# Handing every transfer but weights, first loads and last stores from SyncE's queue to GpSimd's

## The chip, the cores and the metric

The kernel runs on one core of a Trainium2 chip. The metric is the device time of one execution in microseconds (us). Within a core, TensorE (PE), VectorE (DVE), ScalarE (ACT), GpSimd (POOL) and SyncE (SP) each work through a list of instructions of their own in a fixed order. An instruction that waits holds up all that stand behind it on its engine. SP only issues transfers; an issue on any engine sets a transfer going and its landing is told by a semaphore.

## The reference

A two-layer decoder trunk runs over 512 prompt tokens and 8 sample tokens, width 1024, all in float32:

```
for l in 0, 1:
    x = x + 0.5 * rms_norm(swiglu(rms_norm(x)))          # FFN A, inner width 2816
    proj = rms_norm(x) @ w_in                            # q f i g | gu gv | su | gates
    a, hgrn_state = hgrn2(xq, xf, xi, xg, state)         # 4 heads, 128x128 state each
    b, v_rows     = gmlp(gu, gv)                         # 128x128 position mixing
    c, s5_state   = s5(su, state)                        # complex diagonal SSM, 512 wide, then GLU
    merged = sum over branches of sigmoid(gates) * (branch @ w_branch)
    x = x + rms_norm(merged @ w_out)
    x = x + 0.5 * rms_norm(swiglu(rms_norm(x)))          # FFN B
```

The outputs are x after layer 1 and the new states of the three mixers for both token groups.

## The kernel before

The activations stay in SBUF, transposed, in two halves of 256 and 264 columns. Every weight matrix is streamed once: `unit` (L95) loads a block of 128x1024 into one of three `raw` buffers (L102, on SP), ACT rounds it to `whi` (L103) and DVE, for a few blocks POOL, makes the rest `wlo` (L107, L237). `mm3` (L118) multiplies each block in three passes (L122, L123, L125), so that PE has some 20,000 of these matmuls, and they are the bulk of the work.

The order of the instructions on each engine is made when the program is built, by a scheduler that reads the Python code and interleaves it; on the chip it is fixed. Side jobs are written as Python generators that are stepped while the main matmuls are laid down (`tick`, L963). Three of them matter here.

- **The tables.** During FFN A of layer 0, `s5_tables` (L533) computes from the S5 parameters 16 sets of four tables (`s5_table`, L641), 8 for each layer. POOL does most of the arithmetic (L504 to L509, L665 to L667, L683 to L688); PE does four small products a set (L695) that need POOL's `er` and `ei` (L667). Each set is stored to DRAM by four transfers (L711), and a load `bc` (L549) brings the input of a later one.
- **The scan.** At the start of each mixer `s5_project` (L735) writes the S5 input to DRAM and reads it back in another layout (L771 to L779). Then `s5_scan` (L781) makes eight steps. Each loads its four tables (`table`, L792 to L796; tables 0, 1 and 2 have one buffer each), PE projects with table 0 (L803), DVE runs the recurrence, POOL fills edge columns of `w` (L827 to L830), and PE multiplies with tables 2 and 1 (L857 to L859). Every second step goes through DRAM once more (L867, L870).
- **The HGRN heads.** `hgrn_head` (L1035) loads sample states and broadcast values (L1118, L1121) and stores new states (L1129, L1186).

All 920 transfers are issued by SP. Besides the weights these are 496: x in and out, the side jobs' loads and stores, and a spill of x at the middle of each layer (L359) that is read back near the mixer's end (L1348).

Of the kernel before, what the change touches and what calls it, by code (L numbers as in the profile page):

```python
# [45 lines left out]
class Trunk:  # L46
# [29 lines left out]
    def load_consts(self):  # L76
        nc, t, c = self.nc, self.t, self.const
        self.mask = c.tile([P, 64 + 3 * SEGS * 32], U8, name="mask")
        with self.tc.tile_pool(name="mkp", bufs=1) as pool:
            m = pool.tile([P, 64 + 3 * SEGS * 32], F32, name="m")  # L80
            nc.sync.dma_start(m, t["level_mask"])
            nc.gpsimd.tensor_copy(self.mask, m)
        self.tri = c.tile([P, P], F32, name="tri")
        nc.sync.dma_start(self.tri, t["tri_mask"])
        self.hg = c.tile([P, DEPTH * 4], F32, name="hg")
        nc.sync.dma_start(self.hg, t["hgrn_norm_g"])
        self.glub = c.tile([P, DEPTH * 8], F32, name="glub")
        nc.sync.dma_start(self.glub, t["glu_b"])


    def gcol(self, l, i, j, half=False):
# [251 lines left out]
    def residual(self, half, r1, y2, x2, pre, spill):  # L343
        nc, v, sl, w = self.nc, self.nc.vector, SL[half], HW[half]
        if pre is not None and half == 0:
            self.new_h()
        acc = self.acc2_room()[:, :, :w] if pre is not None else None
        for q in range(KD // 2):
            t, xs = y2[q][:, :, sl], x2[q][:, :, sl]
            v.tensor_tensor(t, t, r1[:, None].to_broadcast([P, 2, w]), ALU.mult)  # L350
            v.tensor_tensor(xs, t, xs, ALU.add)
            for e in range(2):
                j = 2 * q + e
                if pre is None:
                    nc.sync.dma_start(self.t["y"][j][:, sl], xs[:, e])
                    continue
                self.pre_hi(*pre, half, j)
                if spill is not None:
                    nc.sync.dma_start(spill[j][:, sl], xs[:, e])  # L359
            if pre is not None:  # L360
                yield
        if pre is None:
            return
        for q in range(KD // 2):
            xs = x2[q][:, :, sl]
            self.pre_lo(*pre, half, 2 * q)
# [144 lines left out]
    def lower_bounds(self):  # L511

        nc, c = self.nc, self.const
        with self.tc.tile_pool(name="lbp", bufs=1) as pool:
            z = pool.tile([P, DEPTH, 4], F32, name="lb_z")
            nc.sync.dma_start(z, self.t["lb_logits"])
            e = pool.tile([P, DEPTH, 4], F32, name="lb_e")
            base = pool.tile([P, DEPTH, 4], F32, name="lb_base")
            m = pool.tile([P, 4], F32, name="lb_m")
# [13 lines left out]
    def s5_tables(self, pool):  # L533
# [12 lines left out]

        def load(i):
            bc = pool.tile([P, 4, 2, 32], F32, tag="bc", name="bc", bufs=3)
            nc.sync.dma_start(bc, self.t["s5_bc"][i // 8, i % 8])  # L549
            return bc  # L550

        n = 8 * DEPTH
# [16 lines left out]
    def s5_params(self, pool, NPR, k):  # L569
# [5 lines left out]
        nc.sync.dma_start(lr, t["lam_re"])  # L575
        nc.sync.dma_start(li, t["lam_im"])
        nc.sync.dma_start(ld, t["log_dt"])
        nc.sync.dma_start(k["d"], t["s5_d"])
# [62 lines left out]
    def s5_table(self, pool, l, s, k, rc, bc):  # L641
# [66 lines left out]
                        k["d"][:, cc][:, :, None].to_broadcast([P, 2, P]), ALU.mult)  # L708
        v.tensor_tensor(m3f, m3f, dd, ALU.add)
        for i in range(4):  # L710
            nc.sync.dma_start(dst[i], tb[i])  # L711
        self.tab.append(dst)
        yield

# [20 lines left out]
    def s5_project(self, l, f_block, ev_f):  # L735
# [32 lines left out]
        for m in range(4):  # L768
            d = self.dr.tile([P, 4, NT // 4], F32, tag="ud", name="ud", bufs=4)
            ds = self.dr.tile([P, NS], F32, tag="us", name="us", bufs=4)  # L770
            nc.sync.dma_start(d, ups[m])  # L771
            nc.sync.dma_start(ds, uss[m])
            ub = self.ub[m]
            nc.gpsimd.memset(ub[:, :, 128:], 0.0)
            dv = d.rearrange("(q c) j n -> j c q n", q=4)
            for j in range(4):
                nc.sync.dma_start(ub[32 * j:32 * j + 32, :, :128], dv[j][:, :, :128])
            for j, c in ((3, 128), (0, 136)):
                nc.sync.dma_start(ub[32 * j:32 * j + 32, :, c:c + NS], ds.rearrange("(q c) n -> c q n", q=4))  # L779

    def s5_scan(self, l, pool):  # L781

# [4 lines left out]
        nc.sync.dma_start(st, t["state_s5"][l])  # L787
# [26 lines left out]
        for s in range(n):  # L814
# [49 lines left out]
                self.gelu2(zb[:, lp + a], pt[:, a * NB:(a + 1) * NB], self.tmp, "sil", 2)  # L864
            if lp == 2:
                d = self.dr.tile([P, 4 * NB], F32, tag="zd", name="zd", bufs=4)
                nc.sync.dma_start(d, zb.rearrange("p q n -> p (q n)"))  # L867
                dv = d.rearrange("(j c) (q n) -> q c j n", j=4, q=4)
                for k in range(4):
                    nc.sync.dma_start(zz[32 * k:32 * k + 32], dv[k])  # L870
                z = self.xp.tile([P, 2, NT], F32R, tag="x", name="z")
                zh, zl = z[:, 0], z[:, 1]
                for d0, src in ((lambda a: a[:, :NP].rearrange("p (n j) -> p n j", j=4),
                                 zz[:, :, :128].rearrange("p j n -> p n j")),
                                (lambda a: a[:, NP:], zz[:, 0, 136:144])):
# [8 lines left out]
        for k, (x0, x1, op) in enumerate(((st[:, 0], st[:, 1], ALU.subtract), (st[:, 1], st[:, 0], ALU.add))):  # L884
# [4 lines left out]
        nc.sync.dma_start(t["s5_sample"][l], new)  # L889
        nc.sync.dma_start(t["s5_prompt"][l], fin)  # L890

    def s5_glu(self, l):
        nc, t = self.nc, self.t
# [90 lines left out]
    def hgrn_values(self, l, hh, pool, V):  # L984
# [10 lines left out]
                                     scale=self.rc[:n, i:i + 1])  # L995

        self.tok_proj("w_i", l, hh, evac)
        nc.sync.dma_start(vd, vs)
        for e in range(2):
            V[2 * hh + e] = v4[e], vd[:, e]  # L1000

# [33 lines left out]
    def hgrn_head(self, l, h, V, q0, qs, k, f, sg, pool, last):  # L1035
# [79 lines left out]

        def load(b0):
            st = pool.tile([P, 2, P], F32, tag="st", name="st", bufs=2)
            nc.sync.dma_start(st, t["state_hgrn"][l, h][:, b0:b0 + 2])  # L1118
            vb = pool.tile([P, 2, P], F32, tag="vb", name="vb", bufs=2)
            for b in range(2):  # L1120
                nc.sync.dma_start(vb[:, b], vd[b0 + b].partition_broadcast(P))  # L1121
            loaded.append((st, vb))

        def state(b0):
            st, vb = loaded.pop(0)
            for b in range(2):
                nc.scalar.activation(st[:, b], st[:, b], AF.Copy, scale=fs[:, b0 + b:b0 + b + 1])
                v.scalar_tensor_tensor(st[:, b], vb[:, b], ks[:, b0 + b:b0 + b + 1], st[:, b], ALU.mult, ALU.add)
            nc.sync.dma_start(t["hgrn_sample"][l, h][:, b0:b0 + 2], st)  # L1129
            states.append((b0, st))  # L1130

        def output():
# [47 lines left out]
        for i in range(4):  # L1180
# [5 lines left out]
        nc.sync.dma_start(t["hgrn_prompt"][l, h], S[3])  # L1186
        yield
        po = self.pxt()
        for i in range(4):
# [38 lines left out]
    def gmlp_norm(self, l, pool):  # L1228
        nc, t, vt = self.nc, self.t, self.vt
        v, g = nc.vector, nc.gpsimd  # L1230
        ng, nb = pool.tile([P, 512], F32, name="ng"), pool.tile([P, 512], F32, name="nb")
        nc.sync.dma_start(ng, t["gmlp_ng"][l])
        nc.sync.dma_start(nb, t["gmlp_nb"][l])
        stat = pool.tile([P, 5, 2], F32, name="stat")
        v.memset(stat, 1.0)
        for i in range(5):
# [9 lines left out]
        for i in range(5):  # L1246
# [5 lines left out]
        nc.sync.dma_start(t["gmlp_v"][l], vt[4][:NS])  # L1252

    def gmlp_mix(self, l, pool, fill):

        nc, t, vt = self.nc, self.t, self.vt
        v, g = nc.vector, nc.gpsimd
        ws = pool.tile([P, 4, P], F32, name="ws")
        nc.sync.dma_start(ws, t["gmlp_ws"][l])
        bs = pool.tile([P, 4, P], F32, name="bs")  # L1260
        nc.sync.dma_start(bs, t["gmlp_bs"][l])
        w00 = pool.tile([NS, 4], F32, name="w00")
        nc.sync.dma_start(w00, t["gmlp_w00"][l])
# [31 lines left out]
    def mixer(self, l, xd, finish, ahead):  # L1295
# [46 lines left out]
        with tc.tile_pool(name=f"mh{l}", bufs=KD) as mh:  # L1342
# [180 lines left out]
```

## Time and profile before

| | |
|---|---|
| median of 3 runs | 2705.61 us (2705.0 to 2705.9) |
| the profiled execution | 2704.64 us, of which the span from first to last instruction 2702.8 us |
| PE busy, matmuls | 2640.5 us, 98% |
| DVE, ACT, POOL busy | 59%, 39%, 21% |
| mean granted PE clock | 0.993 |

Busy is the time in which an engine had an instruction running. PE's 98% says that little of the span is left for waits; the shares of the others are means over stages that differ much: POOL is near full in the tables' stage and almost idle in the FFNs.

### The profile page before, as it was taken

What the parts mean: (1) busy time and instruction counts of PE and PEld (TensorE: products, weight loads), DVE (VectorE), ACT (ScalarE), POOL (GpSimd) and SP (SyncE); (2) the same over time, 40 slices, a digit from 0 to 9 for tenths busy, and PEclk for the clock granted to TensorE, in tenths of its full rate; (3) what the DMA queues carried; (4) which work ended last, traced back from release to release, by engine and by line L of the source; (5) the groups of instructions that cost most, each with busy time, mean ns of one, the idle gap of its engine ahead of it and who ended that gap; (6) DMA issues with size and microseconds to landing.
All of it is one profiled execution on the core that took longest, in us unless ns stands there. A gap on an engine that the chain in (4) does not pass through costs nothing.

```text
span 2702.8 us, 53557 instructions
## 1 busy us (share of the span) xinstructions
PE 2640.5 (98%) x21600; PEld 2615.5 (97%) x21600; DVE 1597.4 (59%) x3421; ACT 1062.8 (39%) x2166; POOL 573.1 (21%) x772
## 2 busy tenths in 40 slices
PE   8899999999999999999999999999999999999998
PEld 7899999999999999999999999998999999999998
DVE  8567877886675473344473344679866545534444
ACT  4244454453333453322443323544434335433232
POOL 5478920220021122011121101012100111201010
PEclk9999999999999999999999999999999999999999
DMA  4344453553232413322322232355332233232331
GB/s 140 102 137 150 151 159 113 171 159 96 88 95 87 141 56 95 97 91 95 94 79 87 93 96 89 123 152 169 116 99 90 89 107 111 69 98 88 99 94 48
DMA packets 131704, 291.22 MB, mean 108 GB/s; under 512 B 19024, under 2 KB 59632, under 8 KB 131456
## 3 DMA queue, kind: packets, MB, share of 16 engines
q1 hardware_dynamic: 131456, 287.79, 33.5%
q8 instruction: 170, 2.79, 0.4%
q14 instruction: 78, 0.64, 0.1%
HBM read 257.07 MB, written 30.67 MB: 106 GB/s over the span
## 4 chain that ended last, share of the span: by engine, by line
PE 80%; issue 7%; DVE 6%; POOL 4%; DMA 2%; ACT 1%; SPq 0%; DVEq 0%; POOLq 0%; ACTq 0%
PE mm L122 24%; PE mm L125 24%; PE mm L123 24%; PE mm L956 1%; PE mm L958 1%; PE mm L957 1%; DMA raw<-in_w_in 1%; PE aux L1073 1%; PE aux L279 1%; PE aux L257 1%; PE aux L695 0%; DVE h L317 0%; DVE acc L218 0%; PE aux L803 0%; DMA x<-in_xT 0%
## 5 line engine op out<-in xcount | busy, mean ns | idle before, releaser
L122 PE MATMUL mm<-h,whi 128*128 128x256 f32 (+1 forms) x4224 | 1059.0, 287 | 22.5 <-ACT h L313 7.0
L123 PE MATMUL mm<-h,wlo 128*128 128x256 f32 (+1 forms) x4224 | 1047.8, 284 | 1.9 <-DVE wlo L107 1.9
L122 PEld LDWEIGHTS mm<-h,whi 128*128 128x128 f32 x4224 | 799.8, 189 | 25.5 <-issue 8.2
L123 PEld LDWEIGHTS mm<-h,wlo 128*128 128x128 f32 x4224 | 802.2, 190 | 3.8 <-DVE wlo L107 3.0
L103 ACT CAST whi<-raw 128x1024 fp32r<-128x1024 f32 (+1 forms) x424 | 437.5, 1032 | 515.6 <-PE mm L125 431.4
L107 DVE TENSOR_TENSOR wlo<-raw,whi 128x1024 fp32r<-128x1024 f32 (+1 forms) x399 | 486.7, 1220 | 243.8 <-ACT whi L103 240.1
L125 PE MATMUL mm<-h,whi 128*128 128x256 f32 (+1 forms) x4224 | 596.9, 284 | 0.0
L125 PEld LDWEIGHTS mm<-h,whi 128*128 128x128 f32 x4224 | 544.4, 189 | 0.1
L122 PE MATMUL mm<-hid,whi 128*128 128x256 f32 (+1 forms) x1408 | 349.6, 285 | 3.6 <-ACT hid L115 3.6
L123 PE MATMUL mm<-hid,wlo 128*128 128x256 f32 (+1 forms) x1408 | 347.8, 283 | 0.0
L116 POOL TENSOR_TENSOR hid<-vb,hid 128x256 fp32r<-128x256 f32 (+1 forms) x132 | 132.5, 1004 | 871.8 <-ACT hid L115 858.9
L129 DVE TENSOR_TENSOR va<-mm,r 128x256 f32<-128x256 f32 (+1 forms) x320 | 136.0, 425 | 279.9 <-PE mm L125 274.9
L122 PEld LDWEIGHTS mm<-hid,whi 128*128 128x128 f32 x1408 | 265.8, 189 | 3.9 <-ACT hid L115 3.8
L123 PEld LDWEIGHTS mm<-hid,wlo 128*128 128x128 f32 x1408 | 266.3, 189 | 0.1
L125 PE MATMUL mm<-hid,whi 128*128 128x256 f32 (+1 forms) x1408 | 201.0, 283 | 0.0
L129 DVE TENSOR_TENSOR vb<-mm,r 128x256 f32<-128x256 f32 (+1 forms) x176 | 74.9, 425 | 188.6 <-PE mm L125 188.5
L125 PEld LDWEIGHTS mm<-hid,whi 128*128 128x128 f32 x1408 | 183.0, 189 | 0.0
L115 ACT CAST hid<-vb 128x256 fp32r<-128x256 f32 (+1 forms) x176 | 72.1, 410 | 277.5 <-DVE vb L416 274.2
L414 ACT ACTIVATE sil<-va 128x256 f32<-128x256 f32 (+1 forms) x176 | 73.7, 419 | 148.0 <-DVE va L129 142.1
L447 DVE TENSOR_TENSOR y<-mm,y 128x264 f32<-128x264 f32 (+1 forms) x128 | 54.3, 426 | 112.9 <-PE mm L125 112.3
L416 DVE TENSOR_TENSOR vb<-vb,sil 128x256 f32<-128x256 f32 (+1 forms) x176 | 84.1, 478 | 16.5 <-ACT sil L414 2.5
L958 PE MATMUL mm<-whi,h 128*128 128x256 f32 (+1 forms) x320 | 90.5, 283 | 0.0
(445 smaller groups left out, 3600.5 us busy)
## 6 DMA issues: line engine op xcount, KB each, us to landing
raw<-in_w_up SPq DMA_DIRECT2D x176, 512.0 KB, 3.6
raw<-in_w_in SPq DMA_DIRECT2D x88, 512.0 KB, 3.6
raw<-in_w_down SPq DMA_DIRECT2D x64, 448.0 KB, 3.3
raw<-in_w_down SPq DMA_DIRECT2D x32, 512.0 KB, 3.4
tab<-tb SPq DMA_DIRECT2D x48, 256.0 KB, 2.4
tab<-tab SPq DMA_DIRECT2D x48, 256.0 KB, 2.9
raw<-in_w_branch SPq DMA_DIRECT2D x24, 512.0 KB, 4.0
raw<-in_w_out SPq DMA_DIRECT2D x16, 512.0 KB, 4.0
```

The costliest lines, as they stand in the source:

```text
L103: nc.scalar.copy(hi[:, :n], raw[:, :n])
L107: nc.vector.tensor_tensor(lo[:, :n], raw[:, :n], hi[:, :n].bitcast(F32), ALU.subtract)
L115: nc.scalar.copy(pair[:, 0], src)
L116: (lo_eng or nc.gpsimd).tensor_tensor(pair[:, 1], src, pair[:, 0].bitcast(F32), ALU.subtract)
L122: mm(out, wh, x[:, 0], start=first and k == 0, stop=False)
L123: mm(out, wl, x[:, 0], start=False, stop=False)
L125: mm(out, wh, x[:, 1], start=False, stop=last and k == n - 1)
L129: self.nc.vector.tensor_tensor(dst, p, self.rms(half), ALU.mult)
L414: nc.scalar.activation(s, a, AF.Silu)
L416: nc.vector.tensor_tensor(b, b, s, ALU.mult)
L447: nc.vector.tensor_tensor(ys, pd, ys, ALU.add)
L958: nc.tensor.matmul(p, self.h[k][:, 1, tk], wh, start=False, stop=k == KD - 1)
```

## The change

Every transfer is issued by POOL instead of SP, except `norm_g` (L72), the weights (L102), the first loads of x (L1372) and the last stores of y (L355). Transfers, sizes, buffers and the arithmetic stay. Of the 920 issues 463 move. The diff, cut to one line of each place that the text speaks of (the others are of the same kind):

```
@@ load_consts, lower_bounds, s5_params: the small constants
-            nc.sync.dma_start(m, t["level_mask"])
+            nc.gpsimd.dma_start(m, t["level_mask"])
             nc.gpsimd.tensor_copy(self.mask, m)
...
-        nc.sync.dma_start(ld, t["log_dt"])
+        nc.gpsimd.dma_start(ld, t["log_dt"])
@@ residual
-                    nc.sync.dma_start(spill[j][:, sl], xs[:, e])
+                    nc.gpsimd.dma_start(spill[j][:, sl], xs[:, e])
@@ s5_tables, s5_table
-            nc.sync.dma_start(bc, self.t["s5_bc"][i // 8, i % 8])
+            nc.gpsimd.dma_start(bc, self.t["s5_bc"][i // 8, i % 8])
...
         for i in range(4):
-            nc.sync.dma_start(dst[i], tb[i])
+            nc.gpsimd.dma_start(dst[i], tb[i])
@@ s5_project
-            nc.sync.dma_start(d, ups[m])
-            nc.sync.dma_start(ds, uss[m])
+            nc.gpsimd.dma_start(d, ups[m])
+            nc.gpsimd.dma_start(ds, uss[m])
...
-                nc.sync.dma_start(ub[32 * j:32 * j + 32, :, :128], dv[j][:, :, :128])
+                nc.gpsimd.dma_start(ub[32 * j:32 * j + 32, :, :128], dv[j][:, :, :128])
@@ s5_scan
-            nc.sync.dma_start(tb, x)
+            nc.gpsimd.dma_start(tb, x)
...
-                    nc.sync.dma_start(zz[32 * k:32 * k + 32], dv[k])
+                    nc.gpsimd.dma_start(zz[32 * k:32 * k + 32], dv[k])
@@ hgrn_head
-                nc.sync.dma_start(vb[:, b], vd[b0 + b].partition_broadcast(P))
+                nc.gpsimd.dma_start(vb[:, b], vd[b0 + b].partition_broadcast(P))
@@ mixer
-                nc.sync.dma_start(self.x[j], xd[j])
+                nc.gpsimd.dma_start(self.x[j], xd[j])
```

Since the scheduler builds the order anew, the lists of all engines shift. First POOL's in the tables' stage, one period of it, from a store of set 2 on (names: `tab_2_2` is table 2 of set 2 in DRAM, `tb` its source; numbers at the end are buffers):

```order
+L711 DMA tab_2_2_2086<-tb_2103 128x256
 L688 TENSOR_TENSOR tb_2313<-tt_2316,tt_2317 128x256
+L711 DMA tab_3_3_2296<-tb_2313 128x512
 L665 TENSOR_TENSOR tt_2584<-bar,er 128x256
 L666 TENSOR_TENSOR tt_2585<-bar,ei 128x256
+L549 DMA bc<-in_s_bc 128x256
 L674 MEMSET tb_2312 128x256
+L711 DMA tab_3_1_2294<-tb_2311 128x512
 L667 TENSOR_TENSOR er<-tt_2584,tt_2585 128x256
 L665 TENSOR_TENSOR tt_2584<-bar,ei 128x256
 L666 TENSOR_TENSOR tt_2585<-bar,er 128x256
+L711 DMA tab_3_0_2293<-tb_2310 128x512
```

Five transfers stand now among POOL's arithmetic of each set, which keeps its order; PE's products of this stage (L695) stand where they stood.

Then POOL's list at the start of layer 0's scan, all of it new or moved (`tab_1_0` is table 0 of step 1):

```order
+L777 DMA y<-ud 32x4x128 x4
+L779 DMA y<-us 32x4x8 x2
+L771 DMA ud<-up 128x520
+L772 DMA us<-up 128x8
+L795 DMA tab<-tab_1_0_1852 128x512
+L827 COPY s_new<-w 128x2x16
+L828 MEMSET w 128x4
+L830 COPY w<-s_h_6596 128x4x8
+L795 DMA tab<-tab_2_3_2087 128x512
+L777 DMA y<-ud 32x4x128 x4
+L779 DMA y<-us 32x4x8 x2
+L829 MEMSET w 128x4x8
```

Before, the copies and memsets of the scan stood here with nothing between them. From the first `ud` store on, 58 issues stand ahead of and with the load of table 2 of step 3, and 102 ahead of the last step's edge columns.

Last PE's list where step 1 of the scan begins (L956 to L958 are matmuls of another projection):

```order
 L958 MATMUL mm<-whi,h 8x256
 L956 MATMUL mm<-whi,h 8x256
+L803 MATMUL aux<-y,tab 128x144 x4
+L857 MATMUL aux<-y,tab 128x144
 L957 MATMUL mm<-wlo,h 8x256
 L958 MATMUL mm<-whi,h 8x256
```

The products of step 1 (L803) and the first of step 0 (L857) now stand 43 large matmuls earlier on PE than before; those of steps 2 and 3 (L803) 38 and 20 earlier; L857 of step 3 stands within 3 of its old place.

## Rows read from the trace of the kernel before

**Rows 1.** The page, part 1: busy us (share of the span) and instructions of each engine.
```profile
PE 2640.5 (98%) x21600; PEld 2615.5 (97%) x21600; DVE 1597.4 (59%) x3421; ACT 1062.8 (39%) x2166; POOL 573.1 (21%) x772
```

**Rows 2.** Waits of PE: us in total, times, longest us; the three longest.
```profile
PE mm L122 <- ACT h L313: 7.0, 1, 7.0
PE mm L122 <- DVE va L129: 6.9, 3, 3.1
PE aux L279 <- DVE diag L272: 6.2, 4, 2.4
```

**Rows 3.** Timeline of SP: start us, us, engine, line, operation, tiles, count; single issues.
```profile
156.17 0.43 SPq L711 DMA_DIRECT2D tab<-tb  x1
158.34 0.33 SPq L711 DMA_DIRECT2D tab<-tb  x1
```

**Rows 4.** POOL's groups by line: busy us, mean ns; idle us before, releaser.
```profile
L116 POOL TENSOR_TENSOR hid<-vb,hid 128x256 fp32r<-128x256 f32 (+1 forms) x132 | 132.5, 1004 | 871.8 <-ACT hid L115 858.9 <-issue 12.9
```

**Rows 5.** The page, part 6: issues, KB each, median us from issue to landing.
```profile
tab<-tb SPq DMA_DIRECT2D x48, 256.0 KB, 2.4
tab<-tab SPq DMA_DIRECT2D x48, 256.0 KB, 2.9
...
zd<-y SPq DMA_DIRECT2D x8, 288.0 KB, 2.1
...
tab<-tab SPq DMA_DIRECT2D x16, 128.0 KB, 2.0
```

**Rows 6.** Windows: length; busy us of PE, PEld, DVE, ACT, POOL; clock, DMA share, GB/s.
```profile
143.60:349.50 205.90, 202.17 (x1647) 201.75 (x1647) 162.94 (x313) 94.36 (x274) 177.74 (x266) 0.98 0.46 150
...
474.90:509.90 35.00, 34.49 (x286) 33.43 (x285) 22.94 (x58) 13.55 (x38) 7.36 (x28) 1.00 0.63 190
...
514.00:600.00 86.00, 81.49 (x634) 78.06 (x633) 79.22 (x234) 42.37 (x115) 19.19 (x40) 1.00 0.48 145
...
1784.90:1833.40 48.50, 47.98 (x396) 46.81 (x395) 33.49 (x79) 21.52 (x52) 7.38 (x28) 1.00 0.61 180
```

**Rows 7.** Line L667, the 16 sets' er and ei: min/median/max ns, first and last start.
```profile
L667 POOL TENSOR_TENSOR er<-tt,tt x16: 729/738/1773, 84.8 to 346.4; 128x256 f32<-128x256 f32 x16
L667 POOL TENSOR_TENSOR ei<-tt,tt x16: 732/774/1601, 88.6 to 348.7; 128x256 f32<-128x256 f32 x16
```

**Rows 8.** Timelines of POOL and PE: er of set 1, and the last set's products.
```profile
143.60 0.73 POOL L667 TENSOR_TENSOR er<-tt,tt 128x256 f32<-128x256 f32 x1 [46.17 <-PE aux L695]
...
356.63 0.43 PE L695 MATMUL aux<-rc,er 128*128 128x160 f32 x2
```

**Rows 9.** Timelines of SP and PE in the scan of layer 0.
```profile
449.86 4.73 SPq L359 DMA_DIRECT2D xd<-x  x8
463.46 2.58 SPq L102 DMA_DIRECT2D raw<-in_w_in  x2
466.26 0.33 SPq L771 DMA_DIRECT2D ud<-up  x1
...
501.13 1.14 PE L803 MATMUL aux<-y,tab 128*128 128x144 f32 x8
...
514.58 0.41 PE L857 MATMUL aux<-y,tab 128*128 128x144 f32 x2
```

**Rows 10.** Timelines of SP and PE in the scan of layer 1.
```profile
1784.91 0.33 SPq L771 DMA_DIRECT2D ud<-up  x1
...
1833.43 0.41 PE L857 MATMUL aux<-y,tab 128*128 128x144 f32 x2
```

**Rows 11.** Timelines of SP, ACT and PE where FFN A's first down block begins; and PE at 72 us.
```profile
72.46 0.55 PE L122 MATMUL mm<-h,whi 128*128 128x256 f32 x1 [4.77 <-DVE vb L129]
...
96.20 0.33 SPq L711 DMA_DIRECT2D tab<-tb  x1
96.62 13.37 SPq L102 DMA_DIRECT2D raw<-in_w_down  x6
...
101.64 0.94 ACT L103 CAST whi<-raw 128x896 fp32r<-128x896 f32 x1 [11.09 <-DMA raw<-in_w_down]
...
104.52 0.36 PE L122 MATMUL mm<-h,whi 128*128 128x256 f32 x1 [3.10 <-DVE va L129]
```

**Rows 12.** Waits of SP's queue: us in total, times, longest us.
```profile
SPq L711 <- POOL tb L688: 107.3, 16, 14.3
```

More of the change, by code (lines that the diff above doesn't have):

```diff
@@ L80, in load_consts @@
             m = pool.tile([P, 64 + 3 * SEGS * 32], F32, name="m")
-            nc.sync.dma_start(m, t["level_mask"])
+            nc.gpsimd.dma_start(m, t["level_mask"])
             nc.gpsimd.tensor_copy(self.mask, m)
         self.tri = c.tile([P, P], F32, name="tri")
-        nc.sync.dma_start(self.tri, t["tri_mask"])
+        nc.gpsimd.dma_start(self.tri, t["tri_mask"])
         self.hg = c.tile([P, DEPTH * 4], F32, name="hg")
-        nc.sync.dma_start(self.hg, t["hgrn_norm_g"])
+        nc.gpsimd.dma_start(self.hg, t["hgrn_norm_g"])
         self.glub = c.tile([P, DEPTH * 8], F32, name="glub")
-        nc.sync.dma_start(self.glub, t["glu_b"])
+        nc.gpsimd.dma_start(self.glub, t["glu_b"])
     def gcol(self, l, i, j, half=False):
@@ L515, in lower_bounds @@
             z = pool.tile([P, DEPTH, 4], F32, name="lb_z")
-            nc.sync.dma_start(z, self.t["lb_logits"])
+            nc.gpsimd.dma_start(z, self.t["lb_logits"])
             e = pool.tile([P, DEPTH, 4], F32, name="lb_e")
@@ L574, in s5_params @@
         lr, li, ld, ee = one("lam_r"), one("lam_i"), one("log_dt"), one("ebase")
-        nc.sync.dma_start(lr, t["lam_re"])
-        nc.sync.dma_start(li, t["lam_im"])
-        nc.sync.dma_start(ld, t["log_dt"])
-        nc.sync.dma_start(k["d"], t["s5_d"])
+        nc.gpsimd.dma_start(lr, t["lam_re"])
+        nc.gpsimd.dma_start(li, t["lam_im"])
+        nc.gpsimd.dma_start(ld, t["log_dt"])
+        nc.gpsimd.dma_start(k["d"], t["s5_d"])
         v.memset(ee, math.e)
@@ L776, in s5_project @@
             for j in range(4):
-                nc.sync.dma_start(ub[32 * j:32 * j + 32, :, :128], dv[j][:, :, :128])
+                nc.gpsimd.dma_start(ub[32 * j:32 * j + 32, :, :128], dv[j][:, :, :128])
             for j, c in ((3, 128), (0, 136)):
-                nc.sync.dma_start(ub[32 * j:32 * j + 32, :, c:c + NS], ds.rearrange("(q c) n -> c q n", q=4))
+                nc.gpsimd.dma_start(ub[32 * j:32 * j + 32, :, c:c + NS], ds.rearrange("(q c) n -> c q n", q=4))
     def s5_scan(self, l, pool):
@@ L786, in s5_scan @@
         st = pool.tile([P, 2, 16, NS], F32, name="s5_h0")
-        nc.sync.dma_start(st, t["state_s5"][l])
+        nc.gpsimd.dma_start(st, t["state_s5"][l])
         new = pool.tile([P, 2, 16, NS], F32, name="s5_new")
@@ L866, in s5_scan @@
                 d = self.dr.tile([P, 4 * NB], F32, tag="zd", name="zd", bufs=4)
-                nc.sync.dma_start(d, zb.rearrange("p q n -> p (q n)"))
+                nc.gpsimd.dma_start(d, zb.rearrange("p q n -> p (q n)"))
                 dv = d.rearrange("(j c) (q n) -> q c j n", j=4, q=4)
                 for k in range(4):
-                    nc.sync.dma_start(zz[32 * k:32 * k + 32], dv[k])
+                    nc.gpsimd.dma_start(zz[32 * k:32 * k + 32], dv[k])
                 z = self.xp.tile([P, 2, NT], F32R, tag="x", name="z")
@@ L888, in s5_scan @@
             g.tensor_tensor(new[:, k], new[:, k], t1, op)
-        nc.sync.dma_start(t["s5_sample"][l], new)
-        nc.sync.dma_start(t["s5_prompt"][l], fin)
+        nc.gpsimd.dma_start(t["s5_sample"][l], new)
+        nc.gpsimd.dma_start(t["s5_prompt"][l], fin)
     def s5_glu(self, l):
@@ L997, in hgrn_values @@
         self.tok_proj("w_i", l, hh, evac)
-        nc.sync.dma_start(vd, vs)
+        nc.gpsimd.dma_start(vd, vs)
         for e in range(2):
@@ L1117, in load @@
             st = pool.tile([P, 2, P], F32, tag="st", name="st", bufs=2)
-            nc.sync.dma_start(st, t["state_hgrn"][l, h][:, b0:b0 + 2])
+            nc.gpsimd.dma_start(st, t["state_hgrn"][l, h][:, b0:b0 + 2])
             vb = pool.tile([P, 2, P], F32, tag="vb", name="vb", bufs=2)
             for b in range(2):
-                nc.sync.dma_start(vb[:, b], vd[b0 + b].partition_broadcast(P))
+                nc.gpsimd.dma_start(vb[:, b], vd[b0 + b].partition_broadcast(P))
             loaded.append((st, vb))
@@ L1128, in state @@
                 v.scalar_tensor_tensor(st[:, b], vb[:, b], ks[:, b0 + b:b0 + b + 1], st[:, b], ALU.mult, ALU.add)
-            nc.sync.dma_start(t["hgrn_sample"][l, h][:, b0:b0 + 2], st)
+            nc.gpsimd.dma_start(t["hgrn_sample"][l, h][:, b0:b0 + 2], st)
             states.append((b0, st))
@@ L1185, in hgrn_head @@
                 v.scalar_tensor_tensor(S[i], S[i - 1], T7[:, i:i + 1], til(pd, i), ALU.mult, ALU.add)
-        nc.sync.dma_start(t["hgrn_prompt"][l, h], S[3])
+        nc.gpsimd.dma_start(t["hgrn_prompt"][l, h], S[3])
         yield
@@ L1231, in gmlp_norm @@
         ng, nb = pool.tile([P, 512], F32, name="ng"), pool.tile([P, 512], F32, name="nb")
-        nc.sync.dma_start(ng, t["gmlp_ng"][l])
-        nc.sync.dma_start(nb, t["gmlp_nb"][l])
+        nc.gpsimd.dma_start(ng, t["gmlp_ng"][l])
+        nc.gpsimd.dma_start(nb, t["gmlp_nb"][l])
         stat = pool.tile([P, 5, 2], F32, name="stat")
@@ L1251, in gmlp_norm @@
             e.tensor_tensor(vt[i][:n], vt[i][:n], nb[:n], ALU.add)
-        nc.sync.dma_start(t["gmlp_v"][l], vt[4][:NS])
+        nc.gpsimd.dma_start(t["gmlp_v"][l], vt[4][:NS])
     def gmlp_mix(self, l, pool, fill):
@@ L1258, in gmlp_mix @@
         ws = pool.tile([P, 4, P], F32, name="ws")
-        nc.sync.dma_start(ws, t["gmlp_ws"][l])
+        nc.gpsimd.dma_start(ws, t["gmlp_ws"][l])
         bs = pool.tile([P, 4, P], F32, name="bs")
-        nc.sync.dma_start(bs, t["gmlp_bs"][l])
+        nc.gpsimd.dma_start(bs, t["gmlp_bs"][l])
         w00 = pool.tile([NS, 4], F32, name="w00")
-        nc.sync.dma_start(w00, t["gmlp_w00"][l])
+        nc.gpsimd.dma_start(w00, t["gmlp_w00"][l])
         wd = pool.tile([NS, 4, NS], F32, name="wd")
```

## Prediction

> **What bounds the kernel now.** I read the page's busy shares first: PE is busy in 98% of the span, and no other engine in more than 59% [rows 1]. A kernel like this loses time only where PE must wait, so the second view is PE's waits: the longest single one is 7.0 us, and the largest groups come to some 7 us each [rows 2]. None of the three is on a transfer that the change moves. The change therefore has little to win, and the question is whether it makes PE wait where it doesn't now. POOL is the engine that gets the work, and its mean share of 21% misleads. The third view is windows: from `er` of set 1 to `ei` of set 15 of the tables, 143.6 to 349.5, POOL is busy for 177.7 of 205.9 us [rows 6]. The fourth is the timelines of those places where PE needs something from POOL or from a moved transfer at a fixed point of its own list: the last set's products at 356.6 [rows 8], and in the scan table 0 of step 3 at 501.1 and table 2 of step 3 at 514.6 [rows 9].
>
> **The price of an issue on POOL, X.** All 920 issues are SP's now, so the trace shows none on POOL. The rows nearest below are SP's own single issues, 0.33 and 0.43 us [rows 3]; the nearest above POOL's elementwise multiply of 128x256, 1.004 us in the FFNs [rows 4]. Between them lies the mean POOL instruction, 573.1/772 = 0.74 us [rows 1]. I take 0.74, since on POOL an issue is one more instruction of an engine whose cheap and dear ones average that, and no row tells what POOL's issues would have in common with SP's. A higher bound comes from POOL under DVE's interference: the same `er` takes 738 ns in the median and 1773 at most [rows 7]. If an issue had to wait for one DVE instruction each time (162.9/313 = 0.52 us in the tables' stage [rows 6]), X would be 0.74 + 0.52 = 1.26.
>
> The Trainium skill, "SBUF — State Buffer", section "SBUF: two separate sides", warns that a transfer issued by GpSimd has its descriptors written by GpSimd's own cores, and that these are locked out while VectorE runs one of its two-port copies. Here the spread of `er` in [rows 7] agrees that something holds POOL up now and then, but no run before shows it for an issue. That rule is rival 2 below.
>
> **The tables' stage.** By the order, 68 issues stand among POOL's arithmetic between `er` of set 1 and `ei` of set 15 (five a set, less the last loads, and a few others). POOL's own list there begins at 143.6, after it had been idle for 46.17 us waiting for PE [rows 8]; so what the constants' loads at the start cost POOL vanishes in that idle time. If POOL then never waits, `ei` of set 15 ends at 143.6 + 177.7 + 68 X. PE wants it at 356.6, and PE's places are unmoved, so the lateness is 68 X − 35.3. At 0.74 this is +15.0 us; at 0.33 it is below nothing and hidden (35.3/68 = 0.52 is the point from which it counts); at 1.0 +32.7; at 1.26 +50.4. Lateness of any earlier set is part of the same total. Nothing else of this stage is on PE's way: the stores to DRAM are read some 100 us later, and each `bc` is loaded a set ahead.
>
> **The scan, once in each layer.** The first `ud` store is issued at 466.3. From it on, 58 issues stand ahead of and with the load of table 2 of step 3. With them stand about 28 POOL instructions, 7.4 us [rows 6], and the load takes 2.0 us to land [rows 5]. PE reads it at 514.6 [rows 9], and that product stands within 3 matmuls of its old place. Lateness: 466.3 + 58 X + 7.4 + 2.0 − 514.6 = 58 X − 38.9, at 0.74 +4.0; at 0.67 nothing; at 1.0 +19.1; at 1.26 +34.2. Table 0 of step 3, 41 issues in, is due at 501.1 less the 20 matmuls by which it moved up, at 2640.5/21600 = 0.12 us each [rows 1]: 498.7. With about 4 us of POOL's instructions and 2.9 us to land it gives 466.3 + 30.3 + 6.9 − 498.7 = +4.8, so two estimates agree within 1 us. They are not added: they are points on one chain. To this comes a wait that is new on POOL: `y<-zd` must stand until `zd` has landed, 2.1 us [rows 5], with the next table loads and the edge columns of `w` queued behind it; I add 2 us. So 6 us a layer. Layer 1 has the same distance, 1784.91 to 1833.43, that is 48.5 against 48.3 [rows 9, 10], and about the same POOL work [rows 6]: 12 us for both.
>
> **What comes back.** In FFN A of layer 0, SP waits 107.3 us in total for POOL's table pieces before it may store them [rows 12], with weights queued behind. At 96.20 such a store goes out, the first `w_down` blocks only at 96.62, ACT waits 11.09 us for them and PE then 3.10 [rows 11]. With the stores gone from SP this wait goes: −3.1 us. The 4.77 us of PE at 72.46 end on `vb` of DVE, and I see no transfer behind it; I leave it.
>
> **Edits at nothing, and their cover.** The spill of x: 8 stores, issued by SP from 449.86 on [rows 9], are 5.9 us of POOL at 0.74, inside the 16.4 us before the first `ud` store; without that room 5.9 a layer. Reading x back: 8 issues, 5.9 us, and the spilled x is added only at the mixer's end. The heads: their loads and stores, 16 and one a head, fall where POOL is busy for only 19.2 of 86 us [rows 6], and the PE matmuls that need them stand at each head's end; if the cover failed, each of a head's 4 loads would come X − 0.33 = 0.41 late, 1.6 us a head and 13 for eight. I take nothing, and keep it for the range.
>
> **Sum.** 15.0 + 12.0 − 3.1 = +23.9 on the profiled execution's 2704.64, that is 2728.5. The median lies 1.0 above that execution: 2729.5, rounded 2730.
>
> **Rivals.** Forecast (X from 0.65 to 0.95): 2710 to 2765, chance 0.44.
>
> Rival 1, an issue costs about what POOL's dear multiply does, X = 1.0: 32.7 + 2 × (19.1 + 2) − 3.1 = +71.8, 2777. For it speaks [rows 4], against it that an issue touches no tile. Chance 0.18. The Trainium skill, "DMA: Bandwidth & Descriptors", section "Specifications", gives about 1 us to the first byte on GpSimd's path and 0.6 on SyncE's; read as POOL's own time, an estimate from that page would be this rival's sum. The trace has no row on it.
>
> Rival 2, DVE holds issues up, X = 1.26: 50.4 + 2 × (34.2 + 2) − 3.1 = +119.7, 2825. For it: DVE is busy 79% of the tables' stage and 66% of the scan [rows 6]. Against it: the median `er` is at 738 beside the same DVE load. Chance 0.17, most of it short of the full price.
>
> Rival 3, an issue is as cheap as on SP, X up to 0.52: tables and scan hidden, −3.1 and at most +4 from `zd`: 2702 to 2707, no change. For it: [rows 3]; the transfers themselves are the same. Chance 0.13.
>
> Rival 4, faster: SP, rid of everything that waits, brings the first weights earlier throughout FFN A; both waits of PE there go, 3.10 + 4.77 [rows 11] = −7.9, 2698. It decides only when X is below 0.52, so that nothing is given back, and if the wait at 72.46 has weights behind it. Chance 0.08.
>
> **Numbers.** This kernel's measurement can tell about 0.2%, 5.4 us, from no change. Slower: the forecast, rivals 1 and 2, 0.79. Same: 0.13. Faster: 0.08. The range of 8 in 10 goes from rival 3's middle, 2704, to 2815, short of rival 2's full price, which leaves out half of rivals 2 and 4 and a part of 3.
>
> **What the changed kernel's profile would show.** POOL's rows of DMA issues, with a mean near 0.74 us and POOL's share near (573 + 463 × 0.74)/2730 = 34%; 0.4 or 1.2 there decides among the rivals. PE's waits: at L695 on `er` and `ei` of POOL, some 15 us in total, growing towards the last sets; in each scan some 6 us at L803 and L857 on tables' loads or POOL's `w`. SP issuing `w_down` near 100 us with no wait, and no 3.10 of PE at 104.5. The forecast is wrong if POOL's own arithmetic gets slower beside its issues, if PE's waits fall at the heads, or if the waits on POOL move the clock.

## The result and the profile after

The changed kernel takes 2748.45 us (median of 4 runs, 2744.72 to 2749.26) against 2705.31 for the kernel before beside it: ratio 1.0158, 95% interval 1.0141 to 1.0176. It is 1.6% slower; forecast were 2730 and "slower". The profiled execution took 2749.26, with a span of 2747.5, 44.7 more than before.

The page, part 1, answers to [rows 1]; below it are POOL's dearest groups of issues, from its list by line (busy us, mean ns; idle before, releasers):

```profile
PE 2649.7 (96%) x21600; PEld 2624.1 (96%) x21600; DVE 1640.5 (60%) x3421; ACT 1063.1 (39%) x2166; POOL 800.1 (29%) x1235
```

```profile
L711 POOL DMA_DIRECT2D tab<-tb x64 | 36.2, 567 | 37.6 <-ACT k L699 25.0 <-POOL tb L688 4.7 <-DVE tb L709 3.8
L795 POOL DMA_DIRECT2D tab<-tab x64 | 34.6, 543 | 31.5 <-DVE ta L846 23.7 <-PE aux L803 3.6 <-DVE st L1128 2.5
L1121 POOL DMA_DIRECT2D vb<-vd x64 | 34.4, 541 | 0.0
```

The unknown price X is in the second column: 0.54 to 0.57 us an issue; all 463 together are 255.2 us, mean 0.55. DVE, which got no work, is busy 43 us longer.

Where the time went is read by taking the same L125 matmul in both timelines, counted from the first, which is number 0, and subtracting its start before from its start after:

```
L125 matmul number     45    245    500    600    800   1100   1320   1700   4000   4520   4900
start before, us     38.3  124.0  221.6  267.1  347.0  458.7  619.9  818.1 1666.7 1938.6 2136.4
after - before       -2.9    1.2    7.1   14.6   25.7   25.9   40.7   38.6   38.7   46.0   44.3
```

The first 38 us gain 2.9. From number 45 to 1100 (the tables' stage, FFN A) 28.8 us are lost, in layer 0's mixer (1100 to 1700) 12.7, in layer 1's (4000 to 4900) 5.6, and nothing elsewhere.

Waits are not all of it. PE is idle 34.8 us longer than before (all gaps between its matmuls, 88.7 against 53.9), and its matmuls are busy 9.2 us longer. The second part is the clock. The granted clock has two levels here, 1.00 (2.4 GHz) and 0.50 (1.2 GHz); the mean of 0.989 instead of 0.993 is 61 us at the lower one instead of 37. Of the 28.8 us of the tables' stage 21.0 are PE's idle time, and the lower level lasts 30.7 us there instead of 17.1. Each of its six stretches in the stage begins during one of PE's longer waits or within 1 us of its end. One of them, beside the wait of 5.78 us that ends at 93.1, and the time behind it, in windows (columns as in [rows 6]):

```profile
92.30:99.00 6.70, 5.90 (x27) 5.93 (x28) 5.73 (x12) 3.38 (x6) 0.80 (x2) 0.50 0.50 149
99.20:106.20 7.00, 7.00 (x61) 7.00 (x60) 4.02 (x8) 3.45 (x6) 0.00 (x0) 1.00 0.46 122
```

A matmul takes 5.90/27 = 0.22 us in the first and 0.115 in the second.

The tables' stage in windows, from `er` of set 1 to `ei` of set 15, answers to [rows 6] (length; busy of PE, PEld, DVE, ACT, POOL; clock, DMA share, GB/s):

```profile
144.80:379.00 234.20, 213.27 (x1680) 210.46 (x1679) 200.19 (x318) 95.75 (x279) 198.79 (x334) 0.96 0.40 133
```

POOL is busy for 198.8 us instead of 177.7. Its 68 issues are 38.7 of them (the sum of their durations), so its arithmetic took 17.6 us less than before. DVE went from 162.9 (313 instructions) to 200.2 (318). PE's own matmuls got dearer too: 213.27/1680 = 0.127 us against 0.123, at a clock of 0.96 against 0.98. PE's waits in the stage, 140 to 400 us (us in total, times, longest):

```profile
PE mm L122 <- DVE va L129: 7.4, 6, 2.2
PE mm L122 <- ACT hid L115: 5.1, 1, 5.1
PE aux L695 <- DVE rc L676: 4.4, 2, 2.4
PE mm L122 <- DVE vb L129: 3.0, 2, 2.1
```

Only the second of these kinds was there before (3.6 us). None names `er` or `ei`: PE waits for DVE, and once for ACT. The list of DVE by line shows why (duration min/median/max in ns; first L107 and L676 after; L676 took 625 at most before, L107 1755):

```profile
L107 DVE TENSOR_TENSOR wlo<-raw,whi x399: 1076/1225/9523, 7.0 to 2688.1; 128x1024 fp32r<-128x1024 f32 x168, 128x896 fp32r<-128x896 f32 x32
L676 DVE COPY rc<-nci x16: 182/494/5505, 54.0 to 382.1; 128x64 f32<-128x64 f32 x16
```

Two instructions of L676 take 5.5 us, and one of L107 takes 9.5. The timeline round the first of L676:

```profile
251.36 0.59 POOL L711 DMA_DIRECT2D tab<-tb  x1 [4.68 <-ACT k L699]
251.62 0.28 DVE L700 TENSOR_TENSOR k<-k,aux 128x32 f32<-128x32 f32 x2
251.81 5.47 DVE L676 COPY rc<-nci 128x64 f32<-128x64 f32 x1
251.97 0.63 POOL L683 TENSOR_TENSOR tt<-lor,hir 128x256 f32<-128x256 f32 x1
...
256.52 0.71 POOL L688 TENSOR_TENSOR tb<-tt,tt 128x256 f32<-128x256 f32 x1
257.21 0.41 DVE L129 TENSOR_TENSOR va<-mm,r 128x256 f32<-128x256 f32 x1
...
257.44 0.51 PE L695 MATMUL aux<-rc,ei 128*128 128x160 f32 x2 [2.39 <-DVE rc L676]
257.53 1.26 POOL L711 DMA_DIRECT2D tab<-tb  x2 [0.30 <-POOL tb L688]
```

The copy begins while POOL issues a store and ends when POOL's twelve instructions behind it are through and POOL waits for the first time. L107's 9.5 us, at 82.33, look the same; PE then waits 5.78 us at 93.1, at a matmul that had no wait before. The wait of 3.10 at 104.5 [rows 11], 32 L125 matmuls further on, is gone.

In the scan, the first store of `ud`, the loads of `y` and PE's first products before (the store was issued at 466.26 [rows 9]):

```profile
471.17 1.75 SPq L777 DMA_DIRECT2D y<-ud  x4
473.01 0.85 SPq L779 DMA_DIRECT2D y<-us  x2
475.64 1.14 PE L803 MATMUL aux<-y,tab 128*128 128x144 f32 x8
```

and after, POOL's timeline:

```profile
495.01 0.55 POOL L771 DMA_DIRECT2D ud<-up  x1 [12.79 <-issue]
...
500.34 2.21 POOL L777 DMA_DIRECT2D y<-ud  x4 [2.66 <-DMA ud<-up]
502.55 1.09 POOL L779 DMA_DIRECT2D y<-us  x2
515.68 0.55 POOL L795 DMA_DIRECT2D tab<-tab  x1 [1.75 <-DVE ta L846]
```

A window from that store to the 41st issue:

```profile
495.00:530.50 35.50, 29.27 (x230) 28.41 (x229) 15.77 (x33) 13.01 (x32) 26.66 (x56) 0.90 0.57 168
```

PE's timeline at L803, and its waits at the heads' L1073 in both layers:

```profile
507.81 2.26 PE L803 MATMUL aux<-y,tab 128*128 128x144 f32 x8 [6.24 <-DMA y<-ud]
534.14 0.73 PE L803 MATMUL aux<-y,tab 128*128 128x144 f32 x4 [2.66 <-DMA tab<-tab]
```

```profile
PE aux L1073 <- ACT w L805: 6.7, 2, 3.4
```

The 6.24 us are step 0's products, for whose `y` the trace of before shows no wait, and the 2.66 step 3's, on table 0. In layer 1 the same two places wait 3.25 and 2.60.

### The profile page after: what moved, and what is told of

It is laid out like the page before. It is cut to its first block, busy times and chain, and to the rows that moved or that the text cites. A ratio compares the mean times of both kernels' runs of the same rounds, so it can differ in the third digit from the quotient of the medians.

```text
span 2747.5 us, 53576 instructions
## 1 busy us (share of the span) xinstructions
PE 2649.7 (96%) x21600; PEld 2624.1 (96%) x21600; DVE 1640.5 (60%) x3421; ACT 1063.1 (39%) x2166; POOL 800.1 (29%) x1235
## 4 chain that ended last, share of the span: by engine, by line
PE 70%; DVE 5%; issue 5%; DMA 3%; POOL 2%; ACT 1%; DVEq 0%; POOLq 0%; ACTq 0%; SPq 0%
PE mm L122 22%; PE mm L125 21%; PE mm L123 21%; PE aux L1073 1%; PE aux L279 1%; PE mm L956 1%; PE aux L257 1%; PE mm L957 1%; PE mm L958 1%; DMA st<-in_state_hgrn 0%; DVE y L350 0%; DVE h L317 0%; DMA y<-ud 0%; DVE x L351 0%; DMA ud<-up 0%
## 5 line engine op out<-in xcount | busy, mean ns | idle before, releaser
L107 DVE TENSOR_TENSOR wlo<-raw,whi 128x1024 fp32r<-128x1024 f32 (+1 forms) x399 | 495.8, 1243 | 246.6 <-ACT whi L103 243.8
L125 PE MATMUL mm<-h,whi 128*128 128x256 f32 (+1 forms) x4224 | 595.4, 283 | 0.0
L125 PEld LDWEIGHTS mm<-h,whi 128*128 128x128 f32 x4224 | 543.2, 189 | 0.0
L129 DVE TENSOR_TENSOR va<-mm,r 128x256 f32<-128x256 f32 (+1 forms) x320 | 136.3, 426 | 277.3 <-PE mm L125 271.9
L125 PE MATMUL mm<-hid,whi 128*128 128x256 f32 (+1 forms) x1408 | 200.8, 283 | 0.0
L129 DVE TENSOR_TENSOR vb<-mm,r 128x256 f32<-128x256 f32 (+1 forms) x176 | 74.9, 426 | 189.4 <-PE mm L125 189.4
L125 PEld LDWEIGHTS mm<-hid,whi 128*128 128x128 f32 x1408 | 182.6, 189 | 0.0
L237 POOL TENSOR_TENSOR wlo<-raw,whi 128x1024 fp32r<-128x1024 f32 x25 | 61.3, 2455 | 107.8 <-ACT whi L103 107.8
L956 PE MATMUL mm<-whi,h 128*128 128x256 f32 (+1 forms) x320 | 92.4, 289 | 0.0
```

Source lines behind the costliest of these rows:

```text
L107: nc.vector.tensor_tensor(lo[:, :n], raw[:, :n], hi[:, :n].bitcast(F32), ALU.subtract)
L125: mm(out, wh, x[:, 1], start=False, stop=last and k == n - 1)
L129: self.nc.vector.tensor_tensor(dst, p, self.rms(half), ALU.mult)
L237: self.nc.gpsimd.tensor_tensor(out, a, b, op)
L956: nc.tensor.matmul(p, self.h[k][:, 0, tk], wh, start=k == 0, stop=False)
```

## The experiments

Times are medians beside the kernel before, in brackets the ratio and its interval. What a stage loses is read from one profiled execution of each kernel, by the L125 matmuls as above.

**E1, the tables back on SP.**

```
-            nc.gpsimd.dma_start(bc, self.t["s5_bc"][i // 8, i % 8])
+            nc.sync.dma_start(bc, self.t["s5_bc"][i // 8, i % 8])
...
-            nc.gpsimd.dma_start(dst[i], tb[i])
+            nc.sync.dma_start(dst[i], tb[i])
```

> The changed kernel with the tables' stores (L711) and bc loads (L549) issued by SP again; 383 transfers stay on POOL. In the changed kernel the stretch from 107 to 372 us lost 23.8 us against before. Theory 'POOL in the tables': that loss goes and the 3.1 us at the first down block comes back as a wait, so 2748 - 24 + 3 = about 2727. Rival 'not the tables' issues but something that the whole change does (order, contention of transfers)': no more than 5 us go, 2743 or more.

2725.98 us (1.0078, 1.0060 to 1.0096). The tables' stage is as before: POOL busy 177.8, DVE 163.0, loss −0.5 us from matmul 45 to 1100. What is left, 26 us of span, is in the mixers. So the tables' issues on POOL do cost over 20 us. The order of the instructions on PE, DVE and ACT is not what costs them: in the stage their lists are those of the changed kernel. Only POOL's arithmetic, without the issues, stands in another order.

**E2 and E6, the scan or the heads back on SP, and E5, both.** The edit is E1's, on the lines named.

> The changed kernel with all transfers of the S5 projection and scan (L771, L772, L777, L779, L787, L795, L867, L870) issued by SP again; the tables and the heads stay on POOL. In the changed kernel the two scans lost 13.0 and 5.6 us. Theory 'the scan's issues in series on POOL': both go, 2748 - 18.6 = about 2730. Rival 'POOL's heads' transfers hold the edge columns up, not the scan's own': half of it stays, 2739 or more.

> The changed kernel with only the heads' transfers (L998, L1118, L1121, L1129, L1186) back on SP. The scan's loads stay on POOL, so PE's waits for y at the first L803 (6.2 and 3.2 us) should stay and those further on (L1073, L1178) go: theory 2748 - 6 to - 9 = 2739 to 2742. Rival 'the scan's issues are the whole loss of the mixers': 2746 to 2750. Rival 'the heads' issues are': about 2731.

> The changed kernel with the scan's and the heads' transfers (all of E2, and L889, L890, L998, L1118, L1121, L1129, L1186) on SP; the tables and the side loads stay on POOL. E2 alone made the mixers slower (PE behind L805 of ACT, behind DVE, behind the heads' broadcast loads on POOL). Theory 'scan and heads each pay when their issues wait in POOL's list, and together on SP neither does': the mixers run as before and the tables' loss stays: 2748 - 18 = about 2730. Rival 'the scheduler's new order of the mixers costs it': 2740 or more.

E2: 2753.12 (1.0188, 1.0166 to 1.0209). E6: 2751.71 (1.0169, 1.0148 to 1.0190). E5: 2731.62 (1.0096, 1.0081 to 1.0112). Neither E2 nor E6 won anything, against the first theory of each; E5 met its own. The mixers (matmuls 1100 to 1700, and 4000 to 4900), layer 0 and layer 1, in us:

```
                    lost           PE idle, more than before   PE at the lower clock (before 3.4, 3.4)
changed kernel      12.7   5.6       11.2   4.9                  10.2   6.8
E1, tables on SP    14.6  13.5        7.0   7.9                  23.9  20.5
E2, scan on SP      16.3  16.7        9.1  12.4                  20.5  13.7
E6, heads on SP     14.2  11.2        8.9   8.5                  17.1  10.2
E5, both on SP       1.4  -0.8        0.4  -0.5                   6.8   3.4
```

E1's mixers are, instruction for instruction and in the same order, those of the changed kernel, and yet lost 28 us in its profiled execution instead of 18, with less idle time and more time at the lower clock. So differences of 10 us between rows are not to be read. By PE's idle time the parts don't add: either one on POOL costs about as much as both. In E2 the reason stands in POOL's and DVE's timelines of the first head:

```profile
519.92 2.18 POOL L1121 DMA_DIRECT2D vb<-vd  x4 [4.44 <-DMA vd<-vs]
...
524.80 0.35 DVE L1128 SCALAR_TENSOR_TENSOR st<-vb,ks,st 128x128 f32<-128x128 f32 x1 [4.26 <-DMA vb<-vd]
...
526.74 0.51 PE L857 MATMUL aux<-y,tab 128*128 128x144 f32 x2 [2.96 <-ACT w L805]
```

The head's broadcast loads wait in POOL's list, DVE waits for them, and the scan's own instructions are queued behind on DVE. In E6 PE waits for the scan's loads (4.34 us for `y`, 3.89 for a table). Whether the scheduler's new order costs something in the mixers is not tested by itself: in E5 the mixers' lists of PE, DVE, ACT and POOL's arithmetic are again those of the kernel before, so that the order went back together with the transfers. It can't be all of it, since the longest wait of the changed kernel, 6.24 us, stands at step 0's products, which did not move, and in E2, where step 1's products stand at their old place, the mixers lose as well.

**E3, the copies into rc on ACT.**

```
-        v.tensor_copy(rc[:, 0, :, P:], bc[:, 2])
-        v.tensor_copy(rc[:, 1, :, P:], nci)
+        nc.scalar.copy(rc[:, 0, :, P:], bc[:, 2])
+        nc.scalar.copy(rc[:, 1, :, P:], nci)
```

> The changed kernel with the two copies into rc (L675, L676) done by ACT instead of DVE; nothing else. In the changed kernel two of them took 5.47 and 5.50 us on DVE where before none took over 1 us, each beginning while POOL issued a store and ending with POOL's burst. Theory 'a DVE instruction that begins during a POOL issue is kept out until POOL's burst ends': the two long copies and PE's waits at 257 and near 270 go, unless another DVE instruction takes their place in the burst; 2748 - 5 to - 8 = 2740 to 2743. Rival 'the issue time of POOL alone sets the tables' stage': the time stays within 2 us of 2748.

2739.86 (1.0133, 1.0114 to 1.0151), as the first theory had it; its interval still touches that of the changed kernel (from 1.0141). DVE's busy time in the stage is 183.8, and the stage loses 20.4 us. The four kernels that leave the stage as changed (the changed kernel, E2, E5, E6) lose 28.8, 27.8, 29.2 and 27.4 there, so the gain is clear of the differences between executions. It is not the long copies' alone: E3 takes all 32 copies off DVE, 12.1 us of work even in the kernel before. One other DVE instruction (L665) took the place in a burst, with 4.6 us.

**E4 and E11, the issue and the burst by themselves.**

> None of the reference's work: outputs are zeros; the kernel only measures. Bursts of 12 (or 6) POOL multiplies of 128x256 without a wait between them beside a stream of DVE multiplies (two SBUF inputs), DVE copies, or DVE multiplies with one PSUM input; each burst begins with one store issued by POOL, by SP, or by nobody; four times each. Also six issues in a row on POOL with and without DVE's stream, and six on SP. Theory 'kept out until the burst ends': with the store on POOL some DVE multiply of two SBUF inputs takes about as long as the burst, 5 us or more; with the store on SP or without one none takes over 2 us; with a PSUM input none does. Rival 'plain contention of two busy engines': the longest DVE instruction is the same with the store on POOL, on SP or without it. An issue on POOL: 0.55 us alone; if DVE holds issues up it is longer beside DVE's stream, otherwise the same.

> As E4, none of the reference's work, outputs zeros. Twelve POOL multiplies of 128x256 with one issue each: at the head; in the middle after six; at the head with POOL waiting for its own first multiply after one, or for its sixth after six; at the head and in the middle both. Also memsets in place of the multiplies, and DVE tensor_scalar or scalar_tensor_tensor in place of multiplies. Theory 'DVE gets in only where POOL stands idle after an issue': longest DVE instruction about 8.9 us at the head, 4.8 in the middle, 1.5 with the wait after one, 4.8 with the wait after six, 8.9 with both. Rival 'the issue itself holds the port for as long as its transfer runs (2 us or so)': 2 to 3 us in all of them. Memsets read nothing: no lockout if it is about reading, the same if about the burst.

In both kernels the engines do nothing else. E4's DVE multiplies (min/median/max ns), with the store on POOL, then on SP, then without one:

```profile
L90 DVE TENSOR_TENSOR do<-da,db x104: 408/414/8914, 3.0 to 71.8; 128x256 f32<-128x256 f32 x104
```

```profile
L90 DVE TENSOR_TENSOR do<-da,db x121: 408/414/947, 71.8 to 137.8; 128x256 f32<-128x256 f32 x121
```

```profile
L90 DVE TENSOR_TENSOR do<-da,db x115: 405/416/947, 137.8 to 202.0; 128x256 f32<-128x256 f32 x115
```

In each of the four bursts with the store on POOL one multiply took 8.8 to 8.9 us. The burst, in POOL's timeline, is 8.19 us long:

```profile
39.42 0.58 POOL L106 DMA_DIRECT2D dst<-da  x1 [9.20 <-DVE do L90]
40.03 8.19 POOL L109 TENSOR_TENSOR go<-xa,xb 128x256 f32<-128x256 f32 x12
```

Without an issue the two engines take turns, and the same burst lasts 10.39. Copies were kept out for 8.63 us; multiplies with a PSUM input never (426 ns at most). E11 gave what the first theory asked for: 8.92 at the head, 4.74 in the middle, 1.44 with POOL waiting after one, 4.82 after six, 0.43 beside memsets. With an issue at the head and another in the middle it was 5.12 and then 3.77, not 8.9: DVE gets in at the second issue. Six issues in a row take 0.54 us each beside DVE's multiplies, and the single ones 0.58 beside copies, the same as beside PSUM multiplies.

**E7, POOL's time without the issues.** On E1:

```
+            g.tensor_tensor(dmy, (tb[2] if i == 2 else tb[i][:, 0])[:, :176], k["one"], ALU.mult)
```

> E1 (the tables' stores and bc loads on SP) with a POOL multiply of 128x176 added for each store, reading the table piece that is stored; its result is used by nobody. It takes POOL's time of the 64 issues (some 0.5 to 0.6 us each, 35 us) without any issue. Theory 'the time itself is nearly hidden (35 us of room), and DVE kept out during issues makes most of the 24 us': E1's 2726 plus 0 to 7, 2726 to 2733. Rival 'POOL's time is the loss': 2726 + 18 to 24 = 2744 to 2750.

2743.86 (1.0141, 1.0127 to 1.0155), 18 over E1: the rival's number. The stage loses 17.3 us. The added multiplies are 41.0 us in the window (637 ns in the median), near the issues' 38.7. So most of the loss comes with POOL's time in its order, and the room of 35 us is not there. A dummy is not time alone, though: it waits for its piece as the store did, DVE waits for dummies before it may go on with a piece (15.8 us at the add of L709), and DVE is busy for 173.8 us instead of 163.1 in the stage.

**E12, a memset behind each store.**

```
+            with self.tc.issue_after(ins):
+                g.memset(k["gap"][:, (l * 8 + s) * 4 + i:(l * 8 + s) * 4 + i + 1], 0.0)
```

> The changed kernel with a POOL memset of 128x1 queued behind each of the tables' 64 stores (directly behind for all but the first store of set 0 and a few). In E11 a DVE multiply beside an issue and memsets took 0.43 us: a memset does not keep DVE out. Theory 'DVE gets in at the memset, so the bursts no longer keep it out': the two copies of 5.5 us go, DVE's busy time between er of set 1 and ei of set 15 falls by 15 us or more, and the time by 8 to 12 us, to 2736 to 2740; the first one (9.5 us, set 0) stays. Rival 'a memset so short changes nothing' or 'the lockouts were paid for by faster POOL work and cost nothing': 2746 to 2754.

2753.04 (1.0179, 1.0164 to 1.0194; its runs from 2745.6 to 2756.8). The first theory fell: the longest copy of L676 went from 5.5 to 2.8 us and the 9.5 of L107 was gone, but DVE's busy time in the stage stayed at 202.5 and the time did not fall. In the profiled execution (2746.47) the stage lost 22.4 us, 5 to 7 less than in the four kernels named under E3, and layer 1's mixer 9.3, 4 more than in the changed kernel. What the stage won lies where the 9.5 us had stood: from number 45 to 245 E12 gains 5.0 us, where those four lose 2.9 to 4.1. Behind 245 it loses 27.4, they 23.9 to 25.4, although the copies of 5.5 us are gone.

**E9, ACT instead of POOL.**

> The changed kernel with all 463 moved transfers issued by ACT instead of POOL. ACT shares no port with POOL here and is 39% busy, but its waits for POOL's tables and DVE's states stand ahead of the weights' rounding (L103). Theory 'the loss is POOL's part in it (its time and DVE kept out), not the leaving of SP': no DVE instruction over 3 us in the tables, and less than half of the loss, below 2727; waits of PE behind L103 or L115 of ACT cost what is left. Rival 'any engine with work of its own loses as much by waiting in order': 2740 or more.

2765.54 (1.0222, 1.0208 to 1.0236). The rival's number, and yet not its mechanism in most of the tables' stage: no DVE instruction of the tables took over 2.5 us, as the first theory had it, and from matmul 245 to 1100 only 1.6 us are lost. The first 45 matmuls lose 6.9, those up to 245 another 5.0, the mixers 24.0 and 23.4: there ACT stands before its next copy until the scan's loads may go.

```profile
505.18 0.37 ACT L994 ACTIVATE V<-mm,rcol 128x128 f32<-128x128 f32 x1 [16.15 <-DMA y<-ud]
```

**E8 and E10, only what has room.** E8 is the kernel before with the constants, the spill and the gmlp loads on POOL; E10 adds

```
+            (nc.gpsimd if i == 3 else nc.sync).dma_start(dst[i], tb[i])
```

> The kernel before with only the constants' loads, the spill of x and its reading back, and the gmlp loads on POOL; tables, scan and heads stay on SP. In the changed kernel and in E1 the first 41 us were 2.4 to 2.9 us shorter than before (PE's wait at 34.8 was gone). Theory 'SP rid of the constants pays at the start and these issues cost nothing': 2704 - 2.5 = about 2701.5, a gain of 0.1%. Rival 'each of these costs a little too': 2704 to 2708.

> E8 with one more store a set on POOL: table 3, whose last half POOL itself computes (L688), so that SP no longer waits for POOL there (107.3 us in 16 waits before). 16 issues are 9 us of POOL's time, inside its room. Theory 'time is hidden, SP's first down blocks come earlier': the wait at 101.5 (2.7 us) goes, 2702 - 2.7 = about 2699. Rival 'each issue may keep DVE out for a burst': one or two DVE instructions of 5 to 9 us in the tables and 2702 + 2 to 6 = 2704 to 2708.

E8: 2701.83 (0.9988, 0.9979 to 0.9997). E10: 2700.33 (0.9985, 0.9976 to 0.9994). Both are a little faster than the kernel before, as expected; between the two this measurement can't tell. In E10 the wait at 101.5 is gone and no DVE instruction of the tables takes over 2.7 us, but 3.6 us are given back between matmuls 500 and 600.

## Why the prediction came out as it did

The sign, the place of the largest loss and the range were right; the size was +43 instead of +24, and the working holds up only in part.

- **X.** Taken 0.74, measured 0.55. By the prediction's own formulas this gives 68 × 0.55 − 35.3 = +2 for the tables and a scan wholly hidden, which would have been next to rival 3. Two errors, a price too high and waits put at nothing, worked against each other, and so far it is luck that the time lies in the range.
- **The tables, forecast +15.0, found +28.8.** The step that failed is "if POOL then never waits". The room of 35.3 us was POOL's idle time (28.2) and the last set's slack (7.1); but a store on POOL waits for pieces of ACT and DVE, with POOL's arithmetic behind it (19.5 us for `k` of ACT in the stage), so that POOL was idle for 35.4 us, more than before. E7 shows that 41.0 us more in POOL's list cost 17.3 and not the 6 that the room would leave. And `er` and `ei` were the wrong witnesses: DVE and ACT need POOL's pieces as well, DVE waits in order, and PE's waits end on DVE's L129 and L676.
- **The other 11 us.** What lies between E7's 17.3 and 28.8 comes only with issues on POOL. That an issue followed by POOL arithmetic keeps DVE out is shown (E4, E11). Some 7 of the 11 us lie before number 245, at the one hold of 9.5 us: with it the kernels lose 2.9 to 4.1 us from 45 to 245, E7 and E12, without it, gain 2.6 and 5.0. What the holds behind 245 cost stays open: E3 loses 17.3 us there instead of 24.7, but takes other work off DVE too, and E12 shortened the longest of them without a gain.
- **Rival 2 had the direction wrong.** DVE does not hold POOL's issues up (0.54 us beside its stream); POOL holds DVE up. The Trainium skill, "SBUF — State Buffer", section "SBUF: two separate sides", says that the shared pair of ports goes to whichever instruction starts first and for the whole of it. The trace goes further, and decides: here the hold lasted through twelve instructions of POOL, 8.9 us. The page's warning that DVE starves GpSimd's issues showed in no run.
- **The scan, forecast 6 a layer.** PE's new waits at L803 are 8.9 and 5.8 us. Step 3's table 0, which I costed, has 2.66 and 2.60 of them; the larger part stands at step 0's `y`, which I did not. The step that failed is again that POOL never waits: from the first store of `ud` to the 41st issue POOL is busy for 26.7 us, what the formula gives at 0.55, and idle for 8.8, among others 2.66 until `ud` has landed and 1.75 for DVE.
- **The heads, forecast at nothing.** The whole mixers lost 12.7 and 5.6, and PE waits 6.7 us at the heads' L1073 for the scan's copy L805. E2, E5 and E6 show that the heads' transfers on POOL cost even with the scan's on SP: the cover failed. E2's timelines show one way, DVE's order, which the heads' loads and the scan share; how much the scheduler's new order adds stays open.
- **What comes back, −3.1.** The wait at 104.5 went, and one of 5.78 at 93.1, behind the hold of 9.5 us, ate it up in the changed kernel; in E12, without that hold, 5.0 us did come back. A gain of 2.9 us up to 38 us, which I had not seen, came from the constants' loads: E8, which moves nothing else so early, has 2.0 of it. Rival 4 was right in that SP rid of some transfers gains, 0.1%, but only if the tables, scan and heads stay.
- **The other edits at nothing** cost nothing (E8).
- **The signs.** POOL's share is 29%, not 34. Of the three signs of being wrong, POOL's arithmetic did not get slower but 17.6 us faster, waits at the heads came in part, and the waits did move the clock, which was put at nothing: PE's matmuls took 9.2 of the 44.7 us.

## What to carry to other kernels

Before transfers go to an engine with work of its own, look at what stands behind each issue in that engine's list and what each must wait for; its idle time is no room if it is idle because it waits for the same engines. Chains that meet on a third engine (here scan and heads on DVE) are best moved together or not at all: in these runs either one alone cost about as much as both. On POOL, keep issues out of runs of arithmetic that reads SBUF while a busy DVE reads SBUF too; constants, spills and reloads can go there, and that was worth 0.1% here. Count the clock with the waits: here PE's longer waits also brought matmuls at 0.22 instead of 0.115 us.

## What the runs showed of the hardware

- An issue costs POOL 0.53 to 0.59 us in the changed kernel, and 0.54 to 0.59 in E4 beside DVE's multiplies, beside its copies and alone (once 0.70); nine in ten of SP's 920 before took 0.32 to 0.45. A single store of 128 KB lands 2.0 us (median) after its issue from POOL and 1.7 from SP (E4).
- A DVE instruction with its inputs in SBUF that begins during a POOL issue is kept out through the POOL multiplies behind the issue, until POOL waits or issues again (8.9 us behind twelve, 4.8 behind six; E4, E11). Behind memsets, or with an input in PSUM, it is not (0.43 us). Without the issue the engines take turns: 0.95 us at most.
- In the burst that keeps DVE out, POOL's 128x256 multiply takes 0.72 us; taking turns it takes 0.90 (E4).
